# Gates of the first eight expert chunks copied on chip, and block 1 of the tokens routed inside the expert loop

## The chip, the cores and the metric

The kernel runs on one core of a Trainium2 chip. TensorE (PE, with its weight loads PEld) multiplies; VectorE (DVE), ScalarE (ACT) and GpSimd (POOL) work beside it; SyncE (SP) issues most DMAs, and GpSimd issues the gathers. The metric is the device time in microseconds (us). Three runs of the kernel before gave 1521.78, 1524.98 and 1530.15 us, the median being 1524.98.

## The reference

One decoder layer on x of 512 tokens by 1024. First come two kinds of attention and a LayerNorm. Then follows a product-key expert layer, and the change lies there:

```python
q = (x @ w_query).reshape(b, s_len, PEER_HEADS, 2, PEER_KEY_DIM // 2)
scores = jnp.einsum('bshpc,hpnc->bshpn', q, sub_keys)
top_s, top_i = lax.top_k(scores, PEER_TOPK)          # 16 per half
...
best_s, best_pos = lax.top_k(cand_s, PEER_TOPK)      # 16 of 256, 8 heads
expert_idx = jnp.take_along_axis(cand_i, best_pos, axis=-1)
gates = jax.nn.softmax(best_s, axis=-1)
...
u = jnp.take(expert_u, ib, axis=0)                   # 128 rows for each token
h = jnp.einsum('td,ted->te', xb, u)
act = gb * jax.nn.gelu(h, approximate=False)
y = jnp.einsum('te,ted->td', act, jnp.take(expert_v, ib, axis=0))
```

There are 128 x 128 = 16,384 experts, with a row of 1024 floats each in expert_u and in expert_v. A last LayerNorm closes the layer.

## The kernel before, in words

The 512 tokens are four blocks of 128. Blocks 0 and 1 go through the experts by gathers: for each of 128 choices an indirect DMA on GpSimd's queue fetches one row a token (512 KB, from `peer_u`, later from `peer_v`), and VectorE uses it in one instruction (L636 for u, L645 for v). That is 4 x 128 = 512 gathers, counted by `done`; nine buffers hold them, and up to eight are issued ahead of the one in use, but never past `limit`.

Blocks 2 and 3 (256 tokens, `ND`) go through all 16,384 experts densely, in 128 chunks of 128 experts. For chunk c, h(c) is eight products of `uT` weights (tile `w`, L739) with the tokens; ScalarE applies the Gelu. VectorE multiplies by the gates (L894, L895, from the tiles `gt` and `glast`). The chunk's rows of `peer_v` are split in a high part `vh` (ScalarE, L867) and a low part `vl` (VectorE, L121). y(c) is twelve products (L915) that add to the result. h runs `LEAD` = 30 chunks ahead of y.

The gates of the dense half are made before that, in a stage loop of 64 steps of four tokens (L839 to L849): one-hot tiles on VectorE and ScalarE, a product on PE (L712), and the copy to a tile `stage` (L718). A `stage` holds 16 tokens for all 128 chunks, 1 MB. Fifteen of them go to a DRAM tile `gd` (L721), two DMAs each; the sixteenth stays on chip as `glast`. Two stage buffers take turns. In the loop PE also runs single products of the h chunks (`run_ahead`, L849), and each chunk's first product issues the `uT` load three chunks further on (L761). After it, `gd` is read back in tiles `gt` of 8 chunks each (L822, 960 KB, `CG` = 8).

Each block is routed (choices, gates and expert indices) by a generator `route_steps` of 22 steps on VectorE. Blocks 0, 2 and 3 are routed earlier. Block 1's steps are called `late`: 15 of them run between the stage loop and the expert loop (L882 to L884), the others two at a time in the first chunks of the loop (L980, L981). Only when they are done is `limit` lifted from 256 to 512, and so the gathers of block 1 are allowed.

The expert loop is L976 to L1002, one pass a chunk, in the order written: split and gate products for the next chunks (`split_all`), routing steps, gather uses up to `goal` (a share of the gathers left at the loop's start, about 2.7 a chunk), h(c+30), y(c), and the loads of `w`, `gt` and `v` for later. The part from L830 on has a fixed order: each engine takes its instructions as the code writes them, and SP's queue too. Memory pools that are closed and opened again share addresses; the `v`, `vh`, `vl` and `a` tiles of the loop lie where the stage, routing and one-hot tiles of the stage loop lay.

Of the kernel before, what the change touches and what calls it, by code (L numbers as in the profile page):

```python
# [10 lines left out]
F32 = mybir.dt.float32  # L11
# [4 lines left out]
AF = mybir.ActivationFunctionType  # L16
# [4 lines left out]
P = 128  # L21
# [48 lines left out]
GRP = 16  # L70
NG32 = ND // GRP
CG = 8
# [5 lines left out]
HSTEP = 2  # L78
# [6 lines left out]
GST = 64  # L85
# [5 lines left out]
def build(ctx, nc, tc, a):  # L91
    def open_pool(stack, name, side, bufs=1, space=None):
        kw = {"space": space} if space is not None else {}
        return stack.enter_context(tc.tile_pool(name=name, bufs=bufs, side=side, **kw))
# [7 lines left out]
    rqs = ExitStack()  # L102
# [3 lines left out]
    rq = open_pool(rqs, "rq", "right")  # L106
# [13 lines left out]
    def low(src, parts):  # L120
        nc.vector.tensor_sub(parts[1], src, parts[0].bitcast(F32))  # L121
# [48 lines left out]
    gate1 = keep.tile([P, NSEL], F32, name="gate1")  # L170
    eidx1 = keep.tile([P, NSEL], I32, name="eidx1")
    hg1 = keep.tile([P, NSEL], F32, name="hg1")
    gd = tc.dram_tile([P, P // CG, NG32 - 1, CG, GRP], F32, name="gd")

    xh = xsp.tile([P, KD, S], F32R, name="x2h")
    xl = xsp.tile([P, KD, S], F32R, name="x2l")
# [211 lines left out]
    def head(steps, n):  # L388
        for _ in range(n):
            if next(steps, steps) is steps:  # L390
                return
            yield
# [288 lines left out]
    us, usp, gls, vs, vsp, acts, gts, gate = {}, {}, {}, {}, {}, {}, {}, {}  # L681
# [3 lines left out]
    hot1, hot, hot2, gps, stages = {}, {}, {}, {}, {}  # L685

    def one_hot_b(s):
        if s < NS:
            tb, t = steps[s]
            hot1[s] = gb.tile([P, P, TG], BF16, name="o1b", bufs=GBUF)  # L690
            nc.vector.tensor_tensor(hot1[s], gate[tb][0][:, None, t:t + TG].to_broadcast([P, P, TG]), iob, op=OP.is_equal)  # L691

    def one_hot_2(s):
        if s < NS:
            tb, t = steps[s]
            hot2[s] = gb.tile([P, TG, P], F32, name="o2")
            nc.vector.tensor_tensor(hot2[s], gate[tb][1][:, 0, t:t + TG, None].to_broadcast([P, TG, P]),  # L697
                                    iota[:, None, :].to_broadcast([P, TG, P]), op=OP.is_equal)

    def gated(s):  # L700
        if s < NS:
            tb, t = steps[s]
            o1b = hot1.pop(s)
            hot[s] = gb.tile([P, TG, P], F32, name="o1", bufs=GBUF)
            for j in range(TG):
                nc.scalar.activation(hot[s][:, j], o1b[:, :, j], AF.Copy, scale=gate[tb][1][:, 1, t + j:t + j + 1])  # L706

    def g_mm(s):
        o1, o2 = hot.pop(s), hot2.pop(s)
        gps[s] = bank(("a", "b", "mm", "mm", "mm")[s % 5])  # L710
        for j in range(TG):
            nc.tensor.matmul(gps[s][:, j * P:(j + 1) * P], o2[:, j], o1[:, j], start=True, stop=True)  # L712

    def g_out(s):
        gi, t0 = s * TG // GRP, s * TG % GRP
        if t0 == 0:
            stages[0] = stg.tile([P, P, GRP], F32, name="stage") if gi < NG32 - 1 else glast
        nc.scalar.activation(stages[0][:, :, t0:t0 + TG], gps.pop(s).rearrange("p (j i) -> p i j", j=TG), AF.Copy)  # L718
        if t0 + TG == GRP and gi < NG32 - 1:
            for i in range(0, P, GST):  # L720
                nc.sync.dma_start(gd[:, i // CG:(i + GST) // CG, gi], stages[0][:, i:i + GST].rearrange("p (g c) t -> p g c t", c=CG))  # L721

    def load_u(c):
        if c < P:
            us[c] = wst.tile([P, KD, P], F32, name="w", bufs=WBUF)
            nc.sync.dma_start(us[c], a["uT"][c])

    def gelu(c, ps):
        if c % 2 == 0:
            gls[c // 2] = up.tile([P, 2, ND], F32, name="gl", bufs=LEAD // 2 + 2)  # L730
        nc.scalar.activation(gls[c // 2][:, c % 2], ps[:, :ND], AF.Gelu)  # L731
# [3 lines left out]
    def h_part(c, k0, k1):  # L735
        if k0 == 0:
            hps[c] = ps_h.tile([P, 512], F32, name="h", bufs=2)
        for k in range(k0, k1):
            nc.tensor.matmul(hps[c][:, :ND], us[c][:, k], xf[:, k], start=k == 0, stop=k == KD - 1)  # L739
        if k1 == KD:  # L740
            del us[c]
# [8 lines left out]
    def run_ahead(n):  # L750
        out = None
        for _ in range(n):
            nxt_ = next(ahead, None)
            if nxt_ is None:
                break
            c, k = nxt_
            if c == k == 0:
                for i in range(3):
                    load_u(i)
            if k == 0:  # L760
                load_u(c + 3)  # L761
                if c and c - 1 in hps:
                    out = c - 1
            h_part(c, k, k + 1)
        if out is not None:
            gelu(out, hps.pop(out))
# [40 lines left out]
    rq = open_pool(wqs, "rq", "right")  # L807
# [2 lines left out]
    wqs.close()  # L810
    glast = open_pool(ctx, "gls", "left").tile([P, P, GRP], F32, name="glast")
    gtp = open_pool(ctx, "gtp", "left", 2)
    stg = open_pool(rqs, "stg", "right", 2)
    rq = open_pool(rqs, "rq", "right")
    gb = open_pool(rqs, "gb", "right", 2)
    iob = gb.tile([P, P, TG], BF16, name="iob", bufs=1)
    nc.vector.tensor_copy(iob, iota[:, :, None].to_broadcast([P, P, TG]))
# [1 line left out]
    def load_g(c):  # L819
        if c < P and c % CG == 0:  # L820
            gts[c // CG] = gtp.tile([P, NG32 - 1, CG, GRP], F32, name="gt")
            nc.sync.dma_start(gts[c // CG], gd[:, c // CG])  # L822

    def load_v(c):
        if c >= P:
            return
        vs[c] = vp.tile([P, D], F32, name="v", bufs=4)
        nc.sync.dma_start(vs[c], a["peer_v"][c * P:(c + 1) * P])

    with tc.manual_schedule():  # L830
        for i, _ in enumerate(route_steps(2)):
            if i % 3 == 0:
                run_ahead(KD)
        one_hot_b(0)
        one_hot_b(1)
        gated(0)
# [2 lines left out]
        for s in range(NS):  # L839
            one_hot_b(s + 2)  # L840
            gated(s + 1)
            one_hot_2(s + 1)
            if next(third, third) is third or s > NS - GSTEP:
                for _ in head(gs, 1):
                    pass
            g_mm(s)
            if s:
                g_out(s - 1)
            run_ahead(HSTEP + (s % 4 == 0))  # L849
        g_out(NS - 1)  # L850
        rqs.close()
        vp = open_pool(ctx, "vp", "left", 2)
        rq = open_pool(ctx, "rq", "right")
        load_v(0)
        load_g(0)
        for n in range(1, 4):
            load_v(n)
        def split_v(c, part=3):
            if c < P:
                if part & 1:  # L860
                    k = c % 3 if c >= P - 9 else 0
                    if k:
                        pool, nm, n = ((gat, "g", GB1), (g2[0], "g2", GB2))[k - 1]
                        vsp[c] = [pool.tile([P, D], F32R, name=nm, bufs=n) for _ in range(2)]
                    else:
                        vsp[c] = [vp.tile([P, D], F32R, name="v" + s_, bufs=3) for s_ in "hl"]
                    nc.scalar.activation(vsp[c][0], vs[c], AF.Copy)  # L867
                if part & 2:
                    low(vs.pop(c), vsp[c])
# [10 lines left out]
                pass  # L880
        gelu(LEAD - 1, hps.pop(LEAD - 1))
        late = route_steps(1)  # L882
        for _ in head(late, 15):
            pass  # L884
        split_v(0)
        front.close()
        ps_y = open_pool(ctx, "ps_y", "right", 1, PSUM)
# [88 lines left out]
        for c in range(P - KT):  # L976
            split_all(c)
            goal = min(NG, pre - (-(NG - pre) * spent(0, c) // spent(0, GEND)))
            if limit < NG:
                next(late, None)  # L980
                if next(late, late) is late:  # L981
                    limit = NG
            goal = min(goal, limit)
            if done < goal:
                for _ in gathers(int(goal)):
                    pass
                if done == NG:
                    todo2 = chain(todo2, final(1))
            next(todo2, None)
            h_mm(c + LEAD)  # L990
            for t in range(2):
                y_mm(t, c)
            load_u(c + LEAD + 3)
            load_g(c + 4)
            upto("l", nxt["v"] + 2, load_v)
            if c == P - LEAD:
                nc.scalar.preload_act_table_set("natural_log_exp_and_others")
                todo2 = final(0)
                ln2 = []
                for n in ("ln2_g", "ln2_b"):  # L1000
                    ln2.append(wst.tile([P, D], F32, name="w", bufs=WBUF))
                    nc.sync.dma_start(ln2[-1], a[n].to_broadcast([P, D]))  # L1002
# [49 lines left out]
```

## Time and profile before

| What | Value |
|---|---|
| Median of three runs | 1524.98 us |
| Profiled execution | 1524.15 us |
| its span, first to last instruction | 1522.4 us |
| PE busy | 1382.0 us (91%) |
| VectorE busy | 1237.1 us (81%) |
| ScalarE busy | 531.2 us (35%) |
| DMA over the span | 497.92 MB, mean 327 GB/s |
| q0 (the gathers' queue) | 270.13 MB |
| q1 (SP's queue) | 224.42 MB |
| Mean granted clock of TensorE | 0.955 |

The span is 1.75 us shorter than the profiled execution's time. Busy shares are means over stages with different limits; the windows and single-engine views below part them. In a timeline row the first number is the start, the second the length, and what stands in brackets is the idle time before the row and what ended it. PE, the weight loads and the DMA overlap, so shares don't add up. A DMA row on SP is the issue; the landing comes later and has a view of its own.

### The profile page before, as it was taken

The page shows a single profiled execution, that of the slowest core. Times are in us where ns is not written, and L with a number is a line of the kernel's source. Part 1 is how long each engine was busy: PE and PEld are TensorE (multiplying, and loading weights), DVE is VectorE, ACT ScalarE, POOL GpSimd, SP SyncE. Part 2 cuts the span into 40 slices and gives each one's busy share as a digit, 9 for nine tenths or more (in the row PEclk, how much of TensorE's full clock was granted, in tenths as well). Part 3 has the DMA queues.
Part 4 walks back from the last instruction along what each step waited for, and adds up shares of the span by engine and source line. Part 5 has one row for each costly group of instructions (what it writes and reads, how often), then busy time and mean ns, then how long its engine had stood idle before and what let it go on. Part 6 is the DMA issues. An engine that isn't in the chain of part 4 may idle for free.

```text
span 1522.4 us, 19944 instructions
## 1 busy us (share of the span) xinstructions
PE 1382.0 (91%) x6718; PEld 1124.7 (74%) x6718; DVE 1237.1 (81%) x2473; ACT 531.2 (35%) x1091; POOL 674.4 (44%) x526
## 2 busy tenths in 40 slices
PE   5999989899959995998949999999999999999896
PEld 3759776666628884887838888888788888888685
DVE  4626978768798999898979887778778877888988
ACT  4732344444311111896722222222222222222352
POOL 0000066557675552034615655555556655656400
PEclk9999999979979997998969999999999999999998
DMA  7847489998899874489988999999999999999972
GB/s 274 267 154 232 140 313 323 332 366 277 278 318 394 315 251 167 151 260 388 387 313 314 410 408 409 409 409 409 410 409 409 409 409 410 410 407 409 392 248 91
DMA packets 166374, 497.92 MB, mean 327 GB/s; under 512 B 15584, under 2 KB 50416, under 8 KB 166272
## 3 DMA queue, kind: packets, MB, share of 16 engines
q0 software_dynamic: 74304, 270.13, 46.7%
q1 hardware_dynamic: 90816, 224.42, 40.2%
q10 hardware_dynamic: 1152, 2.10, 0.4%
q8 instruction: 53, 0.87, 0.2%
q14 instruction: 49, 0.40, 0.1%
HBM read 478.77 MB, written 17.83 MB: 326 GB/s over the span
## 4 chain that ended last, share of the span: by engine, by line
DMA 35%; PE 27%; DVE 18%; issue 17%; ACT 2%; POOL 1%; DVEq 0%; SPq 0%; POOLq 0%; ACTq 0%
DMA g<-peer_u,eidx 17%; DMA g<-peer_v,eidx 14%; PE y L915 7%; PE h L739 7%; DMA gd<-stage 4%; PE mm L431 3%; DVE x L645 2%; DVE yg L645 2%; PE h L329 1%; ACT o L706 1%; DVE g L636 1%; POOL g L627 1%; DVE vl L121 1%; DVE o L697 1%; DVE topi L461 1%
## 5 line engine op out<-in xcount | busy, mean ns | idle before, releaser
L627 POOL DMA_INDIRECT g<-peer_u,eidx x256 | 328.3, 1283 | 404.2 <-DVE eidx L601 186.2
L739 PE MATMUL h<-xf,w 128*128 128x256 f32 x2048 | 478.9, 384 | 26.3 <-ACT gl L731 18.7
L627 POOL DMA_INDIRECT g<-peer_v,eidx x256 | 340.2, 1329 | 349.8 <-DVE yg L645 104.8
L739 PEld LDWEIGHTS h<-xf,w 128*128 128x128 f32 x2048 | 389.2, 193 | 81.6 <-ACT gl L731 19.6
L636 DVE SCALAR_TENSOR_TENSOR g<-g,x 128x1024 f32<-128x1024 f32 x256 | 307.8, 1220 | 85.4 <-DMA g<-peer_u,eidx 84.6
L915 PE MATMUL y<-vh,a 128*128 128x512 f32 x928 | 287.7, 415 | 25.2 <-ACT a L901 24.2
L915 PEld LDWEIGHTS y<-vh,a 128*128 128x128 f32 x928 | 174.1, 190 | 69.5 <-ACT a L901 30.6
L645 DVE SCALAR_TENSOR_TENSOR yg<-g,hg,yg 128x1024 f32<-128x1024 f32 x126 | 161.0, 1278 | 26.6 <-DMA g<-peer_v,eidx 26.4
L645 DVE SCALAR_TENSOR_TENSOR x<-g,hg,x 128x1024 f32<-128x1024 f32 x128 | 163.7, 1279 | 21.2 <-DMA g<-peer_v,eidx 20.8
L901 ACT ACTIVATE a<-gl 128x512 fp32r<-128x512 f32 x58 | 36.5, 630 | 412.9 <-DVE gl L895 412.9
L121 DVE TENSOR_TENSOR vl<-v,vh 128x1024 fp32r<-128x1024 f32 x122 | 148.6, 1218 | 5.9 <-ACT vh L867 5.9
L915 PE MATMUL y<-vl,a 128*128 128x512 f32 x464 | 145.3, 395 | 2.2 <-DVE vl L121 2.2
L867 ACT ACTIVATE vh<-v 128x1024 fp32r<-128x1024 f32 x122 | 128.4, 1054 | 23.0 <-PE y L915 12.7
L915 PEld LDWEIGHTS y<-vl,a 128*128 128x128 f32 x464 | 87.0, 190 | 23.2 <-DVE vl L121 4.9
L706 ACT ACTIVATE o<-o1b,sg 128x128 f32<-128x128 bf16 x256 | 83.9, 406 | 3.1 <-DVE o1b L691 2.9
L731 ACT ACTIVATE gl<-h 128x256 f32<-128x256 f32 x128 | 47.9, 375 | 88.4 <-PE h L739 88.3
L124 PE MATMUL mm<-wh,x2h 128*128 128x512 f32 (+1 forms) x160 | 63.3, 403 | 15.4 <-ACT wh L246 9.2
L121 DVE TENSOR_TENSOR wl<-w,wh 128x1024 fp32r<-128x1024 f32 (+1 forms) x56 | 59.7, 1072 | 19.5 <-ACT wh L246 10.2
L125 PE MATMUL mm<-wl,x2h 128*128 128x512 f32 (+1 forms) x160 | 65.7, 411 | 8.8 <-DVE wl L121 8.8
L126 PE MATMUL mm<-wh,x2l 128*128 128x512 f32 (+1 forms) x160 | 63.7, 398 | 0.0
L117 ACT ACTIVATE wh<-w 128x1024 fp32r<-128x1024 f32 x40 | 42.2, 1055 | 37.0 <-PE mm L126 24.0
L712 PEld LDWEIGHTS mm<-o,o 128*128 128x128 f32 x304 | 41.8, 202 | 14.7 <-ACT o L706 12.1
(241 smaller groups left out, 1866.9 us busy)
## 6 DMA issues: line engine op xcount, KB each, us to landing
w<-uT SPq DMA_DIRECT2D x128, 512.0 KB, 8.9
v<-peer_v SPq DMA_DIRECT2D x128, 512.0 KB, 7.5
w<-w_in SPq DMA_DIRECT2D x40, 512.0 KB, 4.7
gd<-stage SPq DMA_DIRECT2D x30, 512.0 KB, 9.0
gt<-gd SPq DMA_DIRECT2D x16, 960.0 KB, 11.1
w<-peer_wq SPq DMA_DIRECT2D x16, 512.0 KB, 4.5
wq<-peer_wq SPq DMA_DIRECT2D x16, 512.0 KB, 6.8
w<-w_out SPq DMA_DIRECT2D x8, 512.0 KB, 4.4
```

Source lines behind the costliest of these rows:

```text
L121: nc.vector.tensor_sub(parts[1], src, parts[0].bitcast(F32))
L124: nc.tensor.matmul(ps, ah, bh, start=first, stop=False, **kw)
L125: nc.tensor.matmul(ps, ah, bl, start=False, stop=False, **kw)
L126: nc.tensor.matmul(ps, al, bh, start=False, stop=last, **kw)
L627: nc.gpsimd.indirect_dma_start(out=u, out_offset=None, in_=a["peer_v" if kind else "peer_u"], in_offset=bass.IndirectOffsetOnAxis(ap=sets[ ...
L636: nc.vector.scalar_tensor_tensor(u, u, 1.0, x, op0=OP.mult, op1=OP.mult, accum_out=hs[:, j:j + 1])
L645: nc.vector.scalar_tensor_tensor(acc, u, hs[:, j:j + 1], acc, op0=OP.mult, op1=OP.add)
L706: nc.scalar.activation(hot[s][:, j], o1b[:, :, j], AF.Copy, scale=gate[tb][1][:, 1, t + j:t + j + 1])
L731: nc.scalar.activation(gls[c // 2][:, c % 2], ps[:, :ND], AF.Gelu)
L739: nc.tensor.matmul(hps[c][:, :ND], us[c][:, k], xf[:, k], start=k == 0, stop=k == KD - 1)
L867: nc.scalar.activation(vsp[c][0], vs[c], AF.Copy)
L915: nc.tensor.matmul(yps[t][hf], s_, w_[:, hf * 512:(hf + 1) * 512], start=c == 0 and n == 0, stop=c == P - 1 and n == len(terms) - 1)
```

## The change

The first eight chunks' gates (the first `CG` rows of each stage tile) no longer go to `gd` and back. The tile `gt` number 0 is taken before the stage loop, and after each of fifteen stages ScalarE copies that part into it. The two writes to `gd` carry 56 and 64 chunks in place of 64 and 64. The first read of `gd` goes. The pools `rq` (routing tiles) and `stg` (stage tiles) change places. `run_ahead` makes one extra product every eighth step in place of every fourth: 8 products of h fewer in the stage loop. The 15 steps of block 1's routing ahead of the loop are gone from there; all 22 run in the loop, two a chunk.

```diff
-    gd = tc.dram_tile([P, P // CG, NG32 - 1, CG, GRP], F32, name="gd")
+    gd = tc.dram_tile([P, P // CG - 1, NG32 - 1, CG, GRP], F32, name="gd")
...
         if t0 + TG == GRP and gi < NG32 - 1:
-            for i in range(0, P, GST):
-                nc.sync.dma_start(gd[:, i // CG:(i + GST) // CG, gi], stages[0][:, i:i + GST].rearrange("p (g c) t -> p g c t", c=CG))
+            for i, e in ((CG, GST), (GST, P)):
+                nc.sync.dma_start(gd[:, i // CG - 1:e // CG - 1, gi], stages[0][:, i:e].rearrange("p (g c) t -> p g c t", c=CG))
+            nc.scalar.activation(gts[0][:, gi], stages[0][:, :CG], AF.Copy)
...
+    rq = open_pool(rqs, "rq", "right")
     stg = open_pool(rqs, "stg", "right", 2)
-    rq = open_pool(rqs, "rq", "right")
...
-            nc.sync.dma_start(gts[c // CG], gd[:, c // CG])
+            if c:
+                nc.sync.dma_start(gts[c // CG], gd[:, c // CG - 1])
...
+        load_g(0)
         one_hot_b(0)
...
-            run_ahead(HSTEP + (s % 4 == 0))
+            run_ahead(HSTEP + (s % 8 == 0))
...
-        load_v(0)
-        load_g(0)
-        for n in range(1, 4):
+        for n in range(4):
             load_v(n)
...
         late = route_steps(1)
-        for _ in head(late, 15):
-            pass
         split_v(0)
```

On SP, at the end of the stage loop before: the last gate writes, the `w` load of chunk 30, then the `v` and `gt` loads, then `w` of chunks 31 to 33.

```order
L721 DMA gd<-stage 128x8x128 x2
L726 DMA w<-uT 128x1024
L828 DMA v<-peer_v 128x1024
L822 DMA gt<-gd 128x1920
L828 DMA v<-peer_v 128x1024 x3
L726 DMA w<-uT 128x1024 x3
```

The same place now; the `w` ahead of the `v` loads is that of chunk 29.

```order
L721 DMA gd<-stage 128x7x128
L721 DMA gd<-stage 128x8x128
L727 DMA w<-uT 128x1024
L830 DMA v<-peer_v 128x1024 x4
L727 DMA w<-uT 128x1024 x4
L830 DMA v<-peer_v 128x1024
```

The `gt` read is gone, and the `w` load of chunk 30 has moved behind the four `v` loads.

On VectorE, just ahead of the first product y(0) before: the end of the 15 routing steps, then the first split and gate products, and the next routing steps.

```order
L574 TENSOR_TENSOR w<-pos,c_small 128x1024
L576 TENSOR_TENSOR w<-w,d_6231 128x1024
L121 TENSOR_TENSOR vl<-v,vh 128x1024
L894 TENSOR_TENSOR gl<-gl,gt 128x2x240
L895 TENSOR_TENSOR gl<-gl,glast 128x2x16
L907 TENSOR_TENSOR a<-gl,a 128x2x256
L121 TENSOR_TENSOR vl<-v,vh 128x1024
L578 TENSOR_REDUCE bo<-w 128x64
```

The same place now, from the last gather use on:

```order
L645 SCALAR_TENSOR_TENSOR x_97<-g,hg,x_97 128x1024
L121 TENSOR_TENSOR vl<-v,vh 128x1024
L894 TENSOR_TENSOR gl<-gl,gt 128x2x240
L895 TENSOR_TENSOR gl<-gl,glast 128x2x16
L907 TENSOR_TENSOR a<-gl,a 128x2x256
L121 TENSOR_TENSOR vl<-v,vh 128x1024
L534 CAST topf<-topi_3507 128x256
L536 CAST topb<-topf 128x128
```

The split and the gate products of chunk 0 now follow the gather uses at once, and the first routing step stands behind the split of chunk 1.

On VectorE, where block 1's indices (`eidx`) are finished, in pass c = 3 of the loop before; the gather uses that follow (L645) are those of block 0.

```order
L907 TENSOR_TENSOR a<-gl,a 128x2x256
L597 TENSOR_TENSOR eq<-eq 128x64x8
L597 TENSOR_TENSOR eq<-eq 128x64x4
L597 TENSOR_TENSOR eq<-eq 128x64x2
L598 TENSOR_TENSOR i_6236<-eq 128x64
L601 SCALAR_TENSOR_TENSOR eidx_102<-i_6235,i_6236 128x128
L645 SCALAR_TENSOR_TENSOR x_97<-g,hg,x_97 128x1024
```

Now the indices are finished in pass c = 11, and the uses behind them (L636) are block 1's.

```order
L121 TENSOR_TENSOR vl<-v,vh 128x1024
L907 TENSOR_TENSOR a<-gl,a 128x2x256
L601 SCALAR_TENSOR_TENSOR eidx_102<-i_6482,i_6483 128x128
L636 SCALAR_TENSOR_TENSOR g,hg_103<-g,x_97 128x1024
L636 SCALAR_TENSOR_TENSOR g_6733,hg_103<-g_6733,x_97 128x1024
L636 SCALAR_TENSOR_TENSOR g_6735,hg_103<-g_6735,x_97 128x1024
L636 SCALAR_TENSOR_TENSOR g_6737,hg_103<-g_6737,x_97 128x1024
L636 SCALAR_TENSOR_TENSOR g_6739,hg_103<-g_6739,x_97 128x1024
L636 SCALAR_TENSOR_TENSOR g,hg_103<-g,x_97 128x1024 x5
L121 TENSOR_TENSOR vl<-v,vh 128x1024
```

Ten uses of block 1's gathers stand in one row ahead of the next split; before, that pass had three.

## Rows read from the trace of the kernel before

**Rows 1.** Chain that ended last: start, length, engine, tile, line, count.

```profile
794.33 4.51 PE y L915 x12
798.85 3.45 PE h L739 x16
...
876.55 2.73 PE y L915 x12
...
919.98 19.81 DMA g<-peer_u,eidx
...
1405.70 2.29 PE y L915 x10
```

**Rows 2.** Windows: length; busy PE, PEld, DVE, ACT, POOL (count); clock, DMA share, GB/s.

```profile
767.00:794.00 27.00, 7.01 (x20) 5.15 (x18) 19.06 (x89) 3.37 (x5) 1.83 (x2) 0.62 0.76 301
794.00:813.00 19.00, 18.67 (x77) 15.75 (x78) 18.05 (x28) 7.14 (x10) 5.82 (x3) 0.91 0.61 200
813.00:837.00 24.00, 24.00 (x110) 20.50 (x109) 23.86 (x28) 6.37 (x10) 16.37 (x13) 1.00 1.01 396
...
1000.00:1100.00 100.00, 97.08 (x437) 81.72 (x436) 78.73 (x125) 25.12 (x40) 54.60 (x43) 1.00 1.03 409
```

**Rows 3.** Timeline of SP's queue, 753 to 776: start, length, issue.

```profile
757.80 3.35 SPq L726 DMA_DIRECT2D w<-uT  x1
772.95 0.35 SPq L828 DMA_DIRECT2D v<-peer_v  x1
773.34 0.42 SPq L822 DMA_DIRECT2D gt<-gd  x1
```

**Rows 4.** DMA issues in 757.2 to 757.6: count, size, us to landing.

```profile
gd<-stage SPq DMA_DIRECT2D x1, 512.0 KB, 17.8
```

**Rows 5.** Timeline of VectorE, 772 to 810.

```profile
773.46 0.29 DVE L534 CAST topf<-topi 128x256 f32<-128x256 uint32 x1 [6.48 <-issue]
...
791.73 1.22 DVE L121 TENSOR_TENSOR vl<-v,vh 128x1024 fp32r<-128x1024 f32 x1
792.87 0.65 DVE L894 TENSOR_TENSOR gl<-gl,gt 128x480 f32<-128x480 f32 x1
793.44 0.18 DVE L895 TENSOR_TENSOR gl<-gl,glast 128x32 f32<-128x32 f32 x1
...
794.31 0.69 DVE L907 TENSOR_TENSOR a<-gl,a 128x512 fp32r<-128x512 f32 x1 [0.70 <-ACT a L901]
...
805.02 1.28 DVE L645 SCALAR_TENSOR_TENSOR x<-g,hg,x 128x1024 f32<-128x1024 f32 x1
806.22 1.27 DVE L645 SCALAR_TENSOR_TENSOR yg<-g,hg,yg 128x1024 f32<-128x1024 f32 x1
```

**Rows 6.** Timeline of PE, 755 to 800.

```profile
759.86 7.94 PE L739 MATMUL h<-xf,w 128*128 128x256 f32 x36
775.41 6.21 PE L739 MATMUL h<-xf,w 128*128 128x256 f32 x16 [7.61 <-DMA w<-uT]
```

**Rows 7.** DMA issues in 772.9 to 773.2.

```profile
v<-peer_v SPq DMA_DIRECT2D x1, 512.0 KB, 5.7
```

**Rows 8.** DMA issues in 775.34 to 775.6.

```profile
w<-uT SPq DMA_DIRECT2D x1, 512.0 KB, 11.3
```

**Rows 9.** Waits in 680 to 761: us in total, times, longest.

```profile
ACT stage L718 <- DMA gd<-stage: 19.1, 6, 5.0
```

**Rows 10.** Timeline of ScalarE, 770 to 800.

```profile
784.69 0.31 ACT L555 ACTIVATE gate<-gate 128x128 f32<-128x128 f32 x1 [15.17 <-DVE gate L554]
```

**Rows 11.** Windows of ten us in the stage loop.

```profile
670.00:680.00 10.00, 10.00 (x69) 9.38 (x69) 10.00 (x15) 10.00 (x31) 6.72 (x6) 1.00 1.04 369
```

**Rows 12.** Timeline of GpSimd, 796 to 862.

```profile
806.57 1.74 POOL L627 DMA_INDIRECT g<-peer_v,eidx  x1 [37.43 <-DVE x L645]
```

**Rows 13.** DMA issues in 806 to 808.

```profile
g<-peer_v,eidx POOLq DMA_INDIRECT x1, 5.6
```

**Rows 14.** DMA issues in 820 to 822.

```profile
g<-peer_v,eidx POOLq DMA_INDIRECT x1, 10.3
```

## The prediction

> **What bounds the kernel now.** I read the page's shares first, then the chain of waits, then a table of windows, then single engines where two stages meet.
>
> The chain [rows 1] shows three regimes. The second half of the kernel is a loop over 128 expert chunks c: PE runs y(c), then h(c+31). It starts at y(0), 794.33; the slow first piece ends at 798.85. From there PE never pauses: y(13) stands at 876.55, and the pieces before it repeat every 6.19 us (3.45 h, 2.73 y). From 919.98 the chain is one gather after another. At 6.19 us a chunk y(97) would have started at 876.55 + 84 x 6.19 = 1396.5; it starts at 1405.70, so the DMA costs PE only 9.2 us.
>
> The windows [rows 2] say why: the DMA moves 409 GB/s when full (1000 to 1100), 396 already in 813 to 837. A chunk asks for one w and one v load (524,288 bytes each), an eighth of a gt load (983,040 bytes), and about 2.7 gathers of 524,288: 2.6 MB, 6.3 us at 409. PE's 6.19 and the DMA's 6.3 are almost equal, so I keep two books: when PE can be at a chunk, and how long the DMA stood unused. A gain counts only as far as it is in both.
>
> Unused before the full state, in us of full DMA: 27 x (1 - 301/409) = 7.1, 19 x (1 - 200/409) = 9.7, 24 x (1 - 396/409) = 0.8, together 17.6 [rows 2].
>
> **The seam before the loop.** The first v load is issued at 772.95 [rows 3]. It waits for the stage tiles' memory, so for the last gd write, issued at 757.3 and landed 17.8 us later, in a full DMA [rows 4]. The first routing step of block 1 waits for the same memory and starts at 773.46; the first vl follows at 791.73, after 15 routing steps in 18.3 us [rows 5]. PE had stopped at 767.8 for w(30) [rows 6]. So VectorE's 15 steps end last here, and they go.
>
> **The change part by part.**
>
> *Stage loop.* Each of 15 stages writes 15/16 of its MB. About ten fall in the full-DMA stretch after 670: 10 x 65,536 bytes = 0.66 MB, 1.6 us at 409. One w load (1.3 us) moves behind the loop too. ScalarE waits 19.1 us for gd writes here [rows 9], which shorter writes can shorten. Against it stand 15 copies of 128x128; the nearest row of that shape takes 0.31 [rows 10], 4.7 us in all. About seven fall where ScalarE and VectorE are both full (10.00 of 10 [rows 11]), 2.2 us with no cover; the rest lies in ScalarE's waits for gd. Bounds: -3 to +4.7. I take -1, because the late, DMA-full part decides when the last gd lands.
>
> *What is late next at the seam.* The new v wait is for the same gd write, so v(0) is issued at about 772.0. Landing takes 5.7 [rows 7]: 777.7. VectorE needs vh (1.05), vl (1.14 to its next row) and the gate products (1.27: two bigger rows overlapped with a small one): it enters the loop at about 781.2 instead of 794.9 [rows 5]. But the slower run_ahead (one extra step in 8, not in 4) leaves 24 pieces of h instead of 16, and so the load of w(30), which was ahead of the v loads on SP, now stands behind four of them. In the old trace the load three places behind gt landed at 775.34 + 11.3 = 786.6 [rows 8], 8.0 us after v(0) with 3.08 MB between: 385 GB/s. Now 4 x 0.524 MB follow v(0): 5.4 us, and three more gathers compete: 2 us. w(30) lands near 785. h(30) takes 3.45 us, or 6.21 after a pause, as it did at 775.41 [rows 6]; with 5, and y(0) at 2.7 to 3.5, h(31) starts near 793.5 against 798.85. **PE gains 5.3 us, not the 18.3 of the removed steps.** Bounds: 0 (w(30) at 790) to 12 (w(30) with v(0)).
>
> *Routing inside the loop.* VectorE now has, from 781.2 to the end of the split in c = 11: 22 routing steps at 18.3/15 = 1.22 (26.8), 21 gather uses at 1.20 (25.2), 12 vl at 1.14 (13.7), 6 gate products at 1.27 (7.6): 73.3 us, so 854.5. PE reaches y(12) at 871.2 - 6.2 = 865, so up to here VectorE stays ahead and the steps are hidden. The exponential's two table loads inside the loop are covered by ScalarE, busy 25 of 100 us there [rows 2].
>
> *The gathers' pause.* Gathers of block 1 are allowed once its indices exist: at c = 3 before, at c = 11 now. Gathers of block 0 run out first: 21 are left at y(0), 8 are issued ahead, so the last is issued in c = 5, near 818, and with eight still to land the DMA stays busy until about 827. Then only loads run: 1.17 MB in 6.19 us, 189 GB/s, for 28 us: 28 x (1 - 189/409) = 15.1 us unused. With 3 at c = 0, which has no gathers, 18 against 17.6 of before. In bytes, gt of the first eight chunks is not read (-2.4 us) and w(30) comes later (+1.3). DMA book: -1 (stage loop) - 1.1 + 0.4 = **-1.7 us**.
>
> *The burst at c = 11.* There the goal rule asks for ten gather uses at once, with no gather under way, and queued behind them on VectorE is the vl that y(13) needs. First landing 5.6 us after issue, as after the old pause of 37.43 [rows 12, 13]; then one per 1.28 (524,288 bytes at 409) to 1.85 (24 us for the 13 issues of the window 813 to 837 [rows 2]); I take 1.4: 854.5 + 0.6 + 5.6 + 14 + 1.2 = 875.9. PE would be at y(13) at 876.55 - 5.3 = 871.2, so it waits 4.7 us. PE book at y(13): -5.3 + 4.7 = **-0.6 us**. Bounds of the burst: 874.7 with 1.28, and 885.1 with a first landing of 10.3 [rows 14] and 1.85, that is -1.9 to +8.6.
>
> On sharing there is a rule. The Trainium skill, page "DMA: Bandwidth & Descriptors", section "Queues, rings and completion order", says that each DMA engine takes turns between the queue rows that have work. Gathers and SP's loads would then get half each in the burst, 2.56 us a gather, ten in 25.6, and y(13) near 887. The 1.85 of 813 to 837, where both kinds were pending, agrees with sharing, but not with a lasting half, since loads stop when their buffers are full.
>
> *The sum.* From y(13) on the chunks are as before; PE then is held by the DMA, whose book says -1.7, and cannot pass its own, -0.6. I take -1 on the profiled execution (1522.4 span, 1524.15 in all): 1523. The median of the runs, 1524.98, is 0.8 higher and well inside the range.
>
> **Rivals.**
>
> *The early start stays (faster).* If the pause hides in the prefetched loads, and w(30) comes sooner than I have it, PE keeps 8 to 12 us at the seam and the burst ends before y(13) is due: 1513 to 1516. For it: 9.2 us of DMA waiting is all that the old loop had. Against it: 409 GB/s from 837 on without a hole, so unused DMA time must come back. Chance 0.2; 1515.
>
> *The burst holds VectorE (slower).* One mechanism at one place: ten gathers in c = 11 share the DMA with loads, land at 10.3 and then every 1.85 us or slower, and y(13) starts 8.6 to 10 us later than before. Nothing later returns it, because the DMA has no spare rate. It decides from about 22 us of burst. For it: the old gathers took that long in a full DMA. Against it: the DMA is half empty when the burst begins, and while PE waits no loads compete. Chance 0.15; 1533.
>
> *The change doesn't give an earlier start at all.* v still waits for the last gd write, and w(30) has moved behind v; if w(30) lands at 790, y(0) stands where it stood, and the burst, then due at y(13) of 876.5, costs nothing more. 1524 to 1527, inside the band of no change. Chance 0.1.
>
> **How the numbers follow.** Forecast 0.55, early start 0.2, burst 0.15, no earlier start 0.1. Half a per cent, 7.6 us, is about what a measurement here can tell from no change: 1517.4 to 1532.6. The forecast and the last rival lie in it, save 0.04 at the fast edge; of the early start three quarters lie beyond it, of the burst nine tenths. Faster 0.19, same 0.67, slower 0.14. The likeliest case alone is 1518 to 1529; with half of each side the range is 1513 to 1533.
>
> **What would show it.** Right: the first vl near 779, h(30) waiting for w(30) until about 785, h(31) near 793; no peer_u gather before about 855; a stretch of some 28 us near 190 GB/s before it; ten uses in a row on VectorE; y(13) within 3 us of 876; the last chunk with h near 1404. Wrong: h(30) running at 775 without a wait; the stage loop ending over 4 us away from 760; a DMA below 400 GB/s after the burst, which would mean that the DMA book does not bind and PE's own book decides; or y(13) past 885.

## The result and the profile after

The changed kernel takes 1534.08 us (median of 20 runs, 1527.8 to 1544.49) against 1525.24 us (20 runs, 1519.12 to 1535.75): ratio 1.0056, 95% interval 1.0038 to 1.0075. It is slower by 8.8 us where I forecast 1523.0 and "no change"; 1534.08 also lies outside the range of 1513 to 1533.

The profiled execution took 1533.29 us, its span 1531.5, that is 9.1 us more than before. First the windows that answer to [rows 2], columns as there:

```profile
767.00:794.00 27.00, 15.06 (x55) 12.35 (x56) 7.33 (x27) 4.43 (x7) 1.03 (x2) 0.70 0.94 352
794.00:813.00 19.00, 19.00 (x88) 16.26 (x87) 18.38 (x60) 6.23 (x9) 9.46 (x6) 1.00 0.74 255
813.00:837.00 24.00, 24.00 (x110) 20.52 (x109) 23.76 (x37) 6.11 (x9) 9.81 (x6) 1.00 1.00 386
837.00:880.00 43.00, 34.34 (x150) 27.45 (x149) 32.20 (x51) 9.33 (x15) 11.66 (x12) 0.99 0.66 238
...
1000.00:1100.00 100.00, 97.94 (x439) 82.97 (x438) 78.19 (x126) 25.24 (x40) 55.46 (x43) 0.99 1.03 409
```

The last column is the loss. The loop's start is better than before (255 GB/s in place of 200), but 837 to 880 has 238 GB/s. The kernel before had 409 there:

```profile
837.00:880.00 43.00, 43.00 (x197) 36.75 (x196) 35.83 (x49) 11.76 (x18) 26.86 (x19) 1.00 1.03 409
```

In full DMA time 767 to 880 leaves unused 27 x (1 - 352/409) = 3.8, 7.2, 1.3 and 18.0 us, together 30.3, against 17.6 before. Up to 1400 nothing gives this back: from 900 on the DMA of both kernels moves 409 GB/s in every stretch of 100 us.

SP's queue at the seam, which answers to [rows 3]:

```profile
751.37 3.37 SPq L721 DMA_DIRECT2D gd<-stage  x2
754.84 10.79 SPq L727 DMA_DIRECT2D w<-uT  x1
776.46 1.77 SPq L830 DMA_DIRECT2D v<-peer_v  x4
```

The last pair of gate writes is issued 3.1 us earlier than before (754.48), but v(0) 3.5 us later. On VectorE the gap is plain, and the indices come 10 us later than I had them (the first of the rows answers to the 791.73 of [rows 5]):

```profile
785.55 1.23 DVE L121 TENSOR_TENSOR vl<-v,vh 128x1024 fp32r<-128x1024 f32 x1 [19.38 <-ACT vh L869]
...
864.44 0.28 DVE L601 SCALAR_TENSOR_TENSOR eidx<-i,i 128x128 int32<-128x128 f32 x1
871.70 1.23 DVE L636 SCALAR_TENSOR_TENSOR g<-g,x 128x1024 f32<-128x1024 f32 x1 [6.99 <-DMA g<-peer_u,eidx]
...
873.63 1.23 DVE L636 SCALAR_TENSOR_TENSOR g<-g,x 128x1024 f32<-128x1024 f32 x1 [0.69 <-DMA g<-peer_u,eidx]
...
877.31 1.22 DVE L636 SCALAR_TENSOR_TENSOR g<-g,x 128x1024 f32<-128x1024 f32 x1 [2.45 <-issue]
...
886.34 1.23 DVE L636 SCALAR_TENSOR_TENSOR g<-g,x 128x1024 f32<-128x1024 f32 x1
...
887.49 1.22 DVE L121 TENSOR_TENSOR vl<-v,vh 128x1024 fp32r<-128x1024 f32 x1
```

VectorE idles for 19.4 us before the loop, about as long as the 15 removed steps took (18.3); later ten uses and their wait hold back the vl of y(13) until 887.49. PE, in the rows that answer to [rows 6] and to the chain's y(13):

```profile
777.58 6.57 PE L740 MATMUL h<-xf,w 128*128 128x256 f32 x16 [13.94 <-DMA w<-uT]
785.51 3.69 PE L740 MATMUL h<-xf,w 128*128 128x256 f32 x16 [1.35 <-ACT vh L869]
788.85 0.81 PE L915 MATMUL y<-vh,a 128*128 128x512 f32 x2
...
874.02 0.81 PE L915 MATMUL y<-vh,a 128*128 128x512 f32 x2
888.77 1.22 PE L915 MATMUL y<-vl,a 128*128 128x512 f32 x2 [13.94 <-issue]
```

y(0) comes 5.5 us earlier than before (794.33). At y(13) PE starts with the high part at 874.02, 2.2 us ahead of the kernel before (876.20 in this view), and then waits 13.94 us for the low part; y(14) starts at 896.22, against 882.39 before. GpSimd shows the pause:

```profile
828.96 1.74 POOL L627 DMA_INDIRECT g<-peer_v,eidx  x1 [3.65 <-DVE x L645]
864.99 0.94 POOL L627 DMA_INDIRECT g<-peer_u,eidx  x1 [34.28 <-DVE eidx L601]
```

and a window on just that stretch, what the DMA then carries:

```profile
830.00:866.00 36.00, 32.51 (x143) 26.23 (x142) 34.10 (x48) 8.00 (x13) 1.64 (x2) 1.00 0.58 194
```

### The profile page after: what moved, and what is told of

Same layout as the page of the kernel before. It is cut to its first block, busy times and chain, and to the rows that moved or that the text cites. A ratio compares the mean times of both kernels' runs of the same rounds, so it can differ in the third digit from the quotient of the medians.

```text
span 1531.5 us, 19950 instructions
## 1 busy us (share of the span) xinstructions
PE 1380.2 (90%) x6718; PEld 1120.4 (73%) x6718; DVE 1235.7 (81%) x2473; ACT 535.7 (35%) x1106; POOL 687.3 (45%) x526
## 4 chain that ended last, share of the span: by engine, by line
DMA 32%; DVE 13%; PE 9%; issue 4%; ACT 3%; POOL 1%; SPq 0%; POOLq 0%; DVEq 0%; ACTq 0%
DMA g<-peer_v,eidx 15%; DMA g<-peer_u,eidx 13%; PE y L915 4%; PE h L740 4%; DMA gd<-stage 3%; DVE vl L121 2%; DMA w<-uT 1%; ACT o L706 1%; DVE yg L645 1%; DVE x L645 1%; POOL g L627 1%; DVE o L697 1%; DVE gl L894 1%; ACT stage L718 1%; DVE o1b L691 1%
## 5 line engine op out<-in xcount | busy, mean ns | idle before, releaser
L627 POOL DMA_INDIRECT g<-peer_v,eidx x256 | 350.0, 1367 | 336.6 <-DVE yg L645 132.3
L636 DVE SCALAR_TENSOR_TENSOR g<-g,x 128x1024 f32<-128x1024 f32 x256 | 307.4, 1220 | 89.1 <-DMA g<-peer_u,eidx 85.7
L645 DVE SCALAR_TENSOR_TENSOR x<-g,hg,x 128x1024 f32<-128x1024 f32 x128 | 163.7, 1279 | 27.1 <-DMA g<-peer_v,eidx 26.9
L645 DVE SCALAR_TENSOR_TENSOR yg<-g,hg,yg 128x1024 f32<-128x1024 f32 x126 | 161.2, 1279 | 19.6 <-DMA g<-peer_v,eidx 18.6
L121 DVE TENSOR_TENSOR vl<-v,vh 128x1024 fp32r<-128x1024 f32 x122 | 148.6, 1219 | 25.1 <-ACT vh L869 25.1
L915 PE MATMUL y<-vl,a 128*128 128x512 f32 x464 | 146.2, 397 | 15.0 <-issue 13.9
L124 PEld LDWEIGHTS mm<-wh,x2h 128*128 128x128 f32 x160 | 31.3, 197 | 24.6 <-ACT wh L246 9.6
```

What stands on the lines that cost most here:

```text
L124: nc.tensor.matmul(ps, ah, bh, start=first, stop=False, **kw)
L627: nc.gpsimd.indirect_dma_start(out=u, out_offset=None, in_=a["peer_v" if kind else "peer_u"], in_offset=bass.IndirectOffsetOnAxis(ap=sets[ ...
L636: nc.vector.scalar_tensor_tensor(u, u, 1.0, x, op0=OP.mult, op1=OP.mult, accum_out=hs[:, j:j + 1])
L645: nc.vector.scalar_tensor_tensor(acc, u, hs[:, j:j + 1], acc, op0=OP.mult, op1=OP.add)
L915: nc.tensor.matmul(yps[t][hf], s_, w_[:, hf * 512:(hf + 1) * 512], start=c == 0 and n == 0, stop=c == P - 1 and n == len(terms) - 1)
```

## The experiments

Three theories. A, the pause: routing all of block 1 in the loop keeps its gathers back until c = 11, and the DMA time unused meanwhile is missing at the end. B, the seam: the slower run_ahead puts the loads of v(0) and w(30) late. C: the copies on ScalarE and the other edits of the stage loop cost. Ratios below are to the kernel before, run on the same chip, with 95% intervals.

**Routing ahead again (e1).** The changed kernel with

```diff
         late = route_steps(1)
+        for _ in head(late, 15):
+            pass
```

> The changed kernel with one edit undone: 15 of block 1's 22 routing steps stand ahead of the loop again. Theory A (the pause: block 1's gathers come at c = 11 in place of c = 3, so the DMA goes unused and ten gathers come in one burst): the steps run in VectorE's idle 19.4 us (766.2 to 785.5 in the changed kernel), because the routing tiles no longer share memory with the stage tiles; y(0) stays near 789, the wait of 13.9 us at y(13) is gone, gathers of u start before 840, and the time is 1516 to 1522. Theory B (the seam: the slower run_ahead puts the loads of v(0) and w(30) late): 1531 to 1536, since the seam is as in the changed kernel. Theory C (the copies on ScalarE and the other stage edits cost): 1531 to 1536.

Measured: 1519.88 us, ratio 0.9970 (0.9947 to 0.9994). This one edit takes some 14 us off the changed kernel and makes it slightly faster than the kernel before. The windows:

```profile
794.00:813.00 19.00, 19.00 (x87) 16.24 (x86) 18.62 (x28) 4.52 (x7) 7.75 (x5) 1.00 0.66 222
...
837.00:880.00 43.00, 43.00 (x197) 36.76 (x196) 35.87 (x53) 11.06 (x18) 27.30 (x19) 1.00 1.03 409
```

No hole after 837. The first step does start where the gather uses end, with nothing to wait for:

```profile
770.01 0.28 DVE L534 CAST topf<-topi 128x256 f32<-128x256 uint32 x1
```

A holds, B and C alone fall. y(0) is at 791.98, though, and not 789: the steps end at 789.2, 4 us after vh was there, and PE waits 4.78 us for w(30), so that h(30) ends only as y(0) starts.

**run_ahead as before (e2).** The changed kernel with `(s % 4 == 0)`.

> The changed kernel with run_ahead's extra product every fourth step again; the routing stays wholly in the loop. Theory A (pause): within 3 us of the changed kernel's 1534, perhaps 1 to 3 lower, with the wait at y(13) still over 10 us. Theory B (seam): the load of w(30) stands ahead of v again, three gathers fewer run before v(0), the first vl starts some 4 us sooner than 785.5 and the time is 1525 or less. Theory C: 1534.

Measured: 1531.06, ratio 1.0017 (0.9990 to 1.0043). The wait near y(13) is 10.38 us and the pause of the gathers stays. The first vl comes at 783.83, 1.7 us sooner than in the changed kernel and not 4. B is at most a small part: this interval and that of the changed kernel just overlap.

**Routing in the loop alone (e4).** The kernel before without the lines `for _ in head(late, 15): pass`.

> The kernel before with one edit alone: the 15 routing steps ahead of the loop are taken out, so all 22 run in the loop. Theory A (pause): slower than before by 5 to 11 us (1530 to 1536), with y(0) earlier by 5 to 12 us and a wait of over 10 us near y(13). Theory B: 1517 to 1525, since the seam loses 18.3 us of VectorE and w(30) is still loaded ahead of v. Theory C: 1517 to 1525.

Measured: 1529.22, ratio 1.0028 (0.9999 to 1.0056). The median is higher, as A says, though the interval just takes in no change. y(0) starts at 777.37, 17 us earlier than before (I expected 5 to 12), in an execution whose v(0) was issued at 764.46 already, and even so the span is 2.6 us longer than before. Its GpSimd waits 30.82 us for the indices and PE 10.13 us near y(13).

**No burst (e5).** The changed kernel with

```diff
-            goal = min(goal, limit)
+            goal = min(goal, limit, done + 4)
```

> The changed kernel, with at most four gather uses in one pass of the loop, so that the ten of c = 11 are spread over some eight passes; the pause of the gathers stays. Two readings of theory A. Unused DMA time decides: the wait at y(13) falls under 8 us, but PE waits more for gathers later, and the time stays 1530 to 1535. The burst on VectorE decides: the 13.9 us at y(13) are saved and stay saved, 1521 to 1526.

Measured: 1531.64, ratio 1.0042 (1.0018 to 1.0066). The longest wait of PE there falls from 13.94 to 4.55 us, and the median by 2.4 only, within the intervals. So the burst is not the main cause: what PE doesn't wait at y(13) it waits later (from 900 to 1400 it is busy for 488.4 us, against 494.1 in the changed kernel). Of the two readings the one of unused DMA time holds.

**Both undone (e3).** 15 steps ahead, and `(s % 4 == 0)`.

> The changed kernel with both edits undone that the runs so far blame: 15 routing steps ahead of the loop, and run_ahead's extra product every fourth step. The book of unused DMA time (the end moves by the DMA time left unused between the stage loop and 880 us, less the bytes saved): gathers of u from c = 3 or 4, w(30) ahead of the v loads, no DMA wait of PE before y(0), and 2 to 6 us below the kernel with the steps alone (1519.9): 1514 to 1518. If run_ahead's pace was only noise: 1518 to 1521.

Measured: 1518.50, ratio 0.9966 (0.9939 to 0.9992): not to be told from e1, and between the two expectations. PE still waited 8.18 us for w(30) before y(0), which I had not expected. run_ahead's pace is not shown to matter here.

**Three steps a pass (e6).** The changed kernel with one more `next(late, None)` a pass.

> The changed kernel with three routing steps a pass in place of two, so that block 1's gathers are allowed at c = 7 or 8 in place of c = 11; all 22 steps stay in the loop. The book of unused DMA time: gathers of block 0 still run out first, at c = 5, but the pause shrinks from 36 us to 12 to 18, some 7 to 10 us of unused DMA time come back, and the time is 1523 to 1528. If it is the 22 steps on VectorE inside the loop that cost, whenever they run (VectorE was late for y(8) to y(11) by 3.5 us): 1533 to 1537, since they come closer together.

Measured: 1529.71, ratio 1.0024 (0.9998 to 1.0049), between both expectations. The wait for the indices falls to 12.74 us, as expected, but VectorE gets later for several y (PE waits 3.62 us at the longest). So this run does not part the pause from the steps' own time on VectorE; how much of the loss is the latter stays open. Its profiled execution, 1536.08, lies 6.4 us above its median: v(0) was issued at 778.72 only.

**Pools as before (e8).** As e1, with `stg` opened before `rq`.

> The changed kernel with 15 routing steps ahead of the loop, and with the stage pool and the routing pool in their old places, so that the routing tiles share addresses with the stage tiles. If memory sharing decides when the steps can begin: the first step waits for the last gate write again and starts within 1 us of v(0)'s issue, not at the end of the gather uses, the first vl is some 4 to 6 us later than with the pools swapped, and the time is 1522 to 1526. If the place of the pools doesn't matter: 1518 to 1521.

Measured: 1520.89, ratio 0.9967 (0.9940 to 0.9994): not to be told from e1. Yet the mechanism is there: the first step waits for the stage memory and starts with v(0), issued at 776.19:

```profile
776.12 0.29 DVE L534 CAST topf<-topi 128x256 f32<-128x256 uint32 x1 [4.05 <-issue]
```

The first vl is at 794.41, against 789.19, as expected; the median does not show it. The intervals are too wide to say that the later start costs nothing: the profiled execution took 1524.4, 3.5 us above the median of its runs.

**Gates alone (e10).** The kernel before with the copy of the gates (and nothing of run_ahead, pools and routing).

> The kernel before with the copy of the gates alone: routing split 15 and 7 as before, pools and run_ahead as before. If the copy is a gain by itself (1.96 MB fewer in a kernel whose second half runs at 409 GB/s: 4.8 us): 1519 to 1523. If the copies on ScalarE eat it: 1524 to 1528.

Measured: 1525.55, ratio 0.9987 (0.9958 to 1.0017). The time lies in the second range, but the kernel before took 1527.46 beside it, so neither a gain nor a cost is shown, and C, the copies' cost, finds no support.

**Ten steps ahead.** Three kernels. e9 is e3 with `head(late, 10)`; e13 is the same once more; e11 is the kernel before with `head(late, 10)` and nothing else.

> As the kernel with both edits undone, but with ten routing steps ahead of the loop in place of 15. Ten steps take some 12 us, about what VectorE waits for v(0); block 1's gathers are allowed at c = 6, when block 0's are just used up. The book: the first vl near 784 in place of 789, no pause over 8 us in the gathers, and 1511 to 1516. If the gathers must be allowed well before block 0's run out: a pause of over 15 us and 1518 to 1524.

Measured: 1514.52, ratio 0.9933 (0.9902 to 0.9965), with no pause over 8 us after the loop's first gathers. The first vl was at 788.69 and not 784, in an execution of 1522.60, the slowest of the eight.

> The kernel with ten routing steps ahead, gates copied, pools swapped and run_ahead as before, once more for its interval and for a second profile: 1511 to 1518, and a span that differs from the kernel before's by the bytes moved by 900 us, divided by 409 GB/s, less the 4.8 us of saved bytes, to within 3 us.

Measured: 1515.19, ratio 0.9925 (0.9901 to 0.9948), the best version together with e9, the same kernel. In its trace VectorE waits for v(0) only 2.29 us, with v(0) issued at 780.73:

```profile
785.70 1.23 DVE L121 TENSOR_TENSOR vl<-v,vh 128x1024 fp32r<-128x1024 f32 x1 [2.29 <-DMA v<-peer_v]
```

> The kernel before with ten routing steps ahead of the loop in place of 15, nothing else. By the book the five steps (6 us) leave the seam, and block 1's gathers, allowed at c = 6, come without a pause over 10 us: 1517 to 1523. If the routing split only pays together with the gates copied and the pools swapped (here the first step still waits for the last gate write): 1523 to 1529.

Measured: 1523.18, ratio 0.9975 (0.9948 to 1.0002): at the border of the two ranges, and not clear of no change. The first step waits 6.28 us for the stage memory there.

**Six steps ahead (e12).**

> The kernel with ten steps ahead, but six: 16 in the loop, block 1's gathers allowed at c = 8, three passes after block 0's can no longer be issued. The book: a pause of 18 to 25 us, about 8 us of unused DMA time more than with ten, and 1518 to 1524. If the pause's length counts only through the wait at y(13), which should vanish here: 1511 to 1516.

Measured: 1519.71, ratio 0.9943 (0.9919 to 0.9967); the interval overlaps that of ten. It has nine steps more in the loop than e3 (0.9966) and is not slower, so these nine show no cost of their own. The pause is 10.01 us, not 18 to 25, since block 0's last gather is issued at 837.91, later than I worked out:

```profile
849.67 1.74 POOL L627 DMA_INDIRECT g<-peer_u,eidx  x1 [10.01 <-DVE eidx L601]
```

**One view for all.** A window from 0 to 900 us gives, in its last column, how fast each kernel's DMA moved on average before the steady stretch. Before, after, e1 and e5:

```profile
0.00:900.00 900.00, 788.75 (x4101) 632.02 (x4102) 727.80 (x1798) 364.36 (x836) 365.38 (x293) 0.93 0.82 291
```

```profile
0.00:900.00 900.00, 774.84 (x4038) 614.47 (x4039) 719.61 (x1787) 364.25 (x846) 371.00 (x290) 0.93 0.81 285
```

```profile
0.00:900.00 900.00, 790.34 (x4118) 631.19 (x4119) 732.18 (x1808) 368.23 (x852) 377.43 (x297) 0.94 0.82 292
```

```profile
0.00:900.00 900.00, 786.98 (x4098) 626.32 (x4099) 725.19 (x1797) 367.39 (x851) 365.21 (x293) 0.94 0.81 288
```

From 900 to 1400 the DMA moves 409 GB/s in all fourteen profiles. So a GB/s less over 900 us must be made up at 409, in 900/409 = 2.2 us. The gate copy saves bytes, as the pages' lines of before and after say:

```profile
DMA packets 166374, 497.92 MB, mean 327 GB/s; under 512 B 15584, under 2 KB 50416, under 8 KB 166272
```

```profile
DMA packets 164310, 495.96 MB, mean 324 GB/s; under 512 B 15568, under 2 KB 48480, under 8 KB 164208
```

1.96 MB, 4.8 us at 409. The book's difference of span is (291 - rate) x 2.2, less 4.8 where the gates are copied:

| Kernel | rate to 900 us, GB/s | book, us | span against 1522.4, us |
|---|---|---|---|
| changed | 285 | +8.4 | +9.1 |
| e1 | 292 | -7.0 | -4.6 |
| e2 | 285 | +8.4 | +10.6 |
| e3 | 292 | -7.0 | -5.7 |
| e4 | 291 | 0 | +2.6 |
| e5 | 288 | +1.8 | +3.1 |
| e6 | 284 | +10.6 | +11.9 |
| e8 | 289 | -0.4 | +0.2 |
| e9 | 290 | -2.6 | -1.6 |
| e10 | 291 | -4.8 | -3.6 |
| e11 | 294 | -6.6 | -5.6 |
| e12 | 288 | +1.8 | +3.1 |
| e13 | 291 | -4.8 | -3.7 |

It holds for each execution to 2.6 us, always from the same side (a rate is rounded to 1.1 us). It says where the time of one execution went, not why. The profiled executions of e9 (1522.60) and e12 (1527.28) are the slowest of theirs, and their DMA had fallen behind even before the seam: up to 767 us it moved 275 and 274 GB/s, against 280 in the kernel before. So compare edits by medians.

The same view places the loss of the changed kernel. Up to 767 us it moved 280 GB/s, as much as the kernel before; from 767 to 900 the two read, before and after:

```profile
767.00:900.00 133.00, 112.67 (x491) 95.31 (x490) 112.14 (x216) 33.16 (x49) 61.18 (x44) 0.91 0.91 355
```

```profile
767.00:900.00 133.00, 103.64 (x440) 85.97 (x441) 101.36 (x202) 29.29 (x44) 47.41 (x38) 0.89 0.84 316
```

39 GB/s over 133 us is 12.7 us at 409, the whole difference in unused time; it arose behind the stage loop.

## Why the prediction was wrong

**The frame held.** "A gain counts only as far as it is in both" books is what happened. The seam's gain was real on PE (y(0) 5.5 us earlier, h(31) at 791.8, where I had 793.5) and worth nothing, because the DMA book was worse by 12.7 us of unused time.

**The step that failed is "The gathers' pause", in its sum of unused DMA time: 18 us, measured 30.3.** Two terms were too small. The pause itself I had as 15.1 us of loss; 837 to 880 left 18.0. Its length was nearly right (37 us from the last gather of block 0 to the first of block 1, 818 to 855, against 36, 829 to 865), but both ends came some ten us later than I had them. I let gathers in flight fill its first 9 us; they filled about seven, not wholly, and the rest moved 165 GB/s where I had 189:

```profile
830.00:836.00 6.00, 6.00 (x29) 5.13 (x28) 5.96 (x6) 0.00 (x0) 0.70 (x1) 1.00 0.95 341
836.00:866.00 30.00, 26.51 (x116) 21.11 (x115) 28.13 (x43) 8.00 (x13) 0.94 (x1) 1.00 0.50 165
```

PE waited there for VectorE and ScalarE, and its chunks took 7.06 us in place of 6.19 (y(8) at 839.58, y(12) at 867.83); a chunk's 1.17 MB of loads in 7.06 us is 166 GB/s. The other term is the loop's first passes. I counted 3 us for c = 0; 767 to 837 left 12.3 unused (3.8, 7.2, 1.3), where VectorE came into the loop late and the first gathers of the loop were issued at 799.3 only.

**The late start came from "What is late next at the seam".** v(0) was issued at 776.46, not 772.0, although the stage loop ended early, and the first vl ran at 785.55, not 779. The chain has another load ahead of that vl, though, w(29) of uT:

```profile
754.84 22.61 DMA w<-uT
...
777.58 6.59 PE h L740 x16
...
784.48 1.06 ACT vh L869
785.55 1.23 DVE vl L121
```

ScalarE makes vh only behind the Gelu of chunk 29 (784.19), as the code writes them, so vh stood behind h(29) and h(29) behind its load; the forecast's way from v(0) to vl left this out. With my landing of 5.7 us v(0) would have been there at 782.2, an estimate: 4.5 us of the delay of vh (784.48, where I had 777.7) are v(0)'s and 2.3 that of w(29). That h(30) ran at 785.51, where I had about 785, is luck, for it came by this path.

Three more gathers go out behind the stage loop now, because the one more chunk of h that run_ahead leaves over takes three gather uses with it. I charged them to w(30), not to the last gate write. From the issue of the last pair of gate writes to that of v(0) the five kernels with the slower pace took 25.1, 23.0, 21.1, 19.2 and 18.9 us, the nine with the old pace 10.7 to 21.0, mean 15.4: a delay of some 6 us, with much scatter. What of it reaches the time the runs did not settle (e2 against the changed kernel 3 us lower, e3 against e1 1.4).

**The burst.** eidx was ready at 864.7 and not 854.5, the first use came 7.0 us later (6.2), and the ten uses took 1.59 us each (1.4): PE waited 13.9 us where I had 4.7. So PE's own book failed too, -0.6 forecast for y(13) and 13.8 measured at y(14); but the span grew by 9.1 only, and e5 shows that without the burst the DMA's book still holds the time. The rule of the Trainium skill that I weighed ("DMA: Bandwidth & Descriptors", "Queues, rings and completion order", engines taking turns between rows) gave 2.56 us a gather for the whole burst. The trace hardly tests it: the first three uses start 1.9 and 3.7 us apart, and the other seven follow at VectorE's own 1.28, while SP issued no load between 868.21 and 888.74.

**The rivals.** The slower one had the right place, sign and price (1533, with a chance of 0.15), but its mechanism only in part: e5 takes the burst away and leaves most of the time. Its last clause, that the DMA has no spare rate to give anything back, was the truth of the case, and it belonged into the forecast, not into a rival. The early start (faster) fell by the same clause. In "no earlier start" the load of w(30) was not the main bound: PE waited until 777.58 for w(29), and h(30) followed at 785.51.

**The stage loop.** Forecast -1, bounds -3 to +4.7; the last gate writes came 3.1 us earlier in the one execution. e10 sets the copy by itself at 0.9987 (0.9958 to 1.0017), no cost seen.

**The size of the chances.** I gave 0.14 to slower. The bounds of the burst alone reached +8.6; had I put bounds on the unused time too, the two together would have widened the slow side.

## What to carry to other kernels

Where two resources run within about 2% of each other, keep a book for each and ask of an edit what it does to the fuller one: here the change cost 9 us, and giving the early permission to gather back (e1) gained 14, though this put 18 us of work back on the path to the loop. When steps are moved off a seam, check what the engine does there instead (VectorE idled 19.4 us), and try to move only as many as don't fit into that gap. With the gates copied, the pools swapped and the old pace of run_ahead, 0, 6, 10 and 15 steps ahead gave 1.0017, 0.9943, 0.9925 to 0.9933 and 0.9966; none is the worst, while ten against six or 15 is not clear, since their intervals overlap. Where the DMA is full from some point to near the end, its mean rate up to that point tells where one execution's time was lost.

## What the runs showed of the hardware

Loads that stand beside a row of gathers land late. In the changed kernel gathers of 512 KB are issued every 1.24 us from 756.21 on, the DMA moves about 410 GB/s, and the w load that SP issued at 754.84 landed 22.6 us later, by the chain above. Its counterpart in the kernel before, the w load issued at 757.80, took 17.5 us; a w load issued at 775.34, with no gather issued beside it, took 11.3 [rows 8].

The seam scatters from one execution to the next. e9 and e13 are the same kernel, and from the last pair of gate writes to v(0) their profiles took 15.3 and 21.0 us; over all fourteen profiles it was 10.7 to 25.1. That the scatter of the whole time (1527.8 to 1544.49 for the changed kernel) comes from there is not shown: the slower of these two profiles, e9, has the shorter seam.
